# Block products of the first MLP: stores on ScalarE's queue, modulation products in the up stage, two buffers for table products, entry loads with places of their own

## The chip, the cores and the metric

The kernel runs on one core of one Trainium2 chip. Its time is device microseconds of one execution; three runs of the kernel before took 3001.24, 3002.39 and 3007.51 us (median 3002.39 us). One more execution was profiled; every duration below comes from it.

## What is computed

Two layers over 1024 latent tokens and 256 context tokens, model width 1024, MLP width 4096, all in float32. Layer 0 mixes tokens by differential attention, layer 1 by a bidirectional S5 state-space layer. Each mixer is followed by a squared-ReLU MLP; each sub-layer has an RMSNorm before and after, and a shift, scale and gate ("modulation") that come from the conditioning vectors. The part that matters here, cut from the reference:

```python
mod_l = jnp.einsum('bd,de->be', sc, ada_w[i]) + ada_b[i]        # six segments of 1024
h = rmsnorm(x, norm_g[i, 2]) * (1.0 + s2) + sh2
x = x + g2 * rmsnorm(sqrelu_mlp(h, mlp_w1[i], mlp_w2[i]), norm_g[i, 3])
# next layer: h = rmsnorm(x, norm_g[1, 0]) * (1.0 + s1) + sh1, then the S5 mixer
def sqrelu_mlp(h, w1, w2):
    return jnp.einsum('btf,fd->btd', jnp.square(jax.nn.relu(jnp.einsum('btd,df->btf', h, w1))), w2)
```

## The kernel before

A float32 product is made as three TensorE products of split operands (high times high, high times low, low times high; `mm3`, L132 to L134). The split is a ScalarE copy (L137) and a VectorE subtraction (L138). All DMAs but a few at the start are issued by SyncE, through the helper at L80, in one queue in program order.

The program is written stage by stage, but a scheduler with a timing model of its own then lays out each engine's instructions: an instruction goes where that model has it ready, not where the code emits it. Background work is given as generators in `self.bg`; `step()` advances the first of them.

**Up stage** (`mlp0_up`). The hidden width is done in pairs of 128-column blocks, by products of sums (Strassen's scheme: seven products `A11, S1, S2, S4, S3, A12, A22` for a pair instead of eight). ScalarE copies and squares, VectorE adds. For the blocks from `CONV` = 8 on, the hidden blocks and their sums are stored to `Hd[0..6]`, 84 stores of 320 KB: 12 pairs times seven kinds. Beside it GpSimd forms the sums of the rows of `mlp_w2` (L1546 to L1549, `sum_rows`): two row blocks are loaded, combined, and stored to `Td`. In the background stands `ada(0, 5)`: for one modulation segment eight loads of 512 KB, four small matmuls each (L208), then the end of the segment (L222 to L236); and `rows_out` (L286 to L288), which writes the layer's modulation to `rowd` in DRAM.

**Down stage** (`mlp0_start`, `mlp0_blocks`, `mlp0_down`). 84 block products ("ops") are worked off. Each has a load from `Hd` and one from `mlp_w2` or `Td` into one of a few raw places (`oraw`, `op_load`), a split into one of 14 slots (`op_prepare`), and 15 matmuls. Places and slots lie in tiles H, W, RW and RD; RW and RD get their memory only when the up stage's pool is free. After the ops come the groups of the plain hidden blocks (`mlp0_group`, additions L1497). When both parts of a token tile are added, `m0_tile` runs its end: ScalarE squares (L1830), the products with modulation rows (L1831), the residual (L1842), the modulation (L1850); then four transposes (L1817) put it into U, which the S5 layer reads. The rows come from `rowd`.

In the background of the down stage stand `s5_phases`, then `s5_tables` (32 steps: loads, VectorE and GpSimd products, transposes on TensorE at L1189 and their copy L1190, a product L1199, its copy L1201 into `Ks`, and every second step four stores of `Ks` to `kd`), with four `lags`, each of which issues 32 DMAs from `ktd` to `recd`; then `ada(1, 0)`, `ada(1, 1)` and `rows_out(1)`. After each unit of ops `step` is called (L1711), and `mlp0_down` drains what is left. The first S5 product is at L1925 and needs U and the tables in `recd`.

Of the kernel before, what the change touches and what calls it, by code (L numbers as in the profile page):

```python
# [6 lines left out]
F32 = mybir.dt.float32  # L7
F32R = mybir.dt.float32r
I32 = mybir.dt.int32
AF = mybir.ActivationFunctionType  # L10
# [60 lines left out]
class Prog:  # L71
# [140 lines left out]
    def ada_steps(self, l, seg, acc, raw):  # L212
        for k in range(8):
            w = raw.next()
            self.ada_load(w, l, seg, k)
            self.ada_product(w, k, acc)
            yield
        self.ada_end(l, seg, acc)
        yield

# [929 lines left out]
    def s5_tables(self, o, w, acc):  # L1150
# [9 lines left out]
        t4, t2, Ks = shaped(t, (4, 9, 16)), shaped(t[:, 0:512], (4, 8, 16)), self.wv(w + 7, 2, 128)  # L1160
# [34 lines left out]
        def products(i):  # L1195
            tb_, W, q = ins[i % 4][2], Wr[i % 3], todo[i]
            d, x0 = q // 16, 4 * q
            for j in range(4):
                nc.tensor.matmul(acc[32 * j : 32 * j + 32, 0:128], tb_[:, j],  # L1199
                                 W[:, j, d : d + 8].rearrange("p i c -> p (i c)"), start=True, stop=True)  # L1200
            nc.scalar.activation(Ks[:, q % 2], acc[:, 0:128], AF.Copy)  # L1201
            if q % 2:
                for j in range(4):
                    dst = self.kd[x0 - 4 : x0 + 4].rearrange("(y j) c n -> j c y n", j=4)[j]
                    self.dma(dst, Ks[32 * j : 32 * j + 16])
# [323 lines left out]
    def mlp0_up(self):  # L1529
# [5 lines left out]
        self.bg = [self.ada(0, 5, acc), self.rows_out(0, acc)]  # L1535
# [5 lines left out]
        def store(n, p, t):  # L1541
            self.dma(self.Hd[self.KINDS.index(n)][p - self.CONV // 2], t)

        def sum_rows(p):
            (b11, b12), (b21, b22) = ((r[:, 0:512], r[:, 512:1024]) for r in rows)
            g(b11, b12, b11, ALU.subtract)  # L1546
            g(b12, b22, b12, ALU.subtract)
            g(b22, b22, b11, ALU.subtract)
            g(b21, b21, b22, ALU.subtract)  # L1549
            for j in range(2):  # L1550
                self.dma(self.Td[p - self.CONV // 2, j], rows[j])

        for p in range(self.HEAD // 2, 16):
            conv = 2 * p < self.CONV
            if p < 15:
                for j in range(2):
                    self.dma(rows[j], self.I["mlp_w2"][0, 128 * (2 * p + 2 + j) : 128 * (2 * p + 2 + j) + 128])
# [3 lines left out]
            for j in range(2):  # L1561
# [7 lines left out]
                while later:  # L1569
                    later.pop(0)()  # L1570

            def emit(j, gr, t):
# [28 lines left out]
                if (j, gr) == (1, 1) and p < 15:  # L1601
                    sum_rows(p + 1)
# [8 lines left out]
    def mlp0_start(self):  # L1611
# [11 lines left out]
        self.raw = Ring([self.fv(40, 1024), self.fv(44, 1024)])  # L1623
        acc = self.bank(3)
        self.bg = [self.s5_phases(40), self.s5_tables(40, 0, acc)] + [self.ada(1, seg, acc) for seg in (0, 1)]
        self.bg.append(self.rows_out(1, acc))
# [8 lines left out]
        slots = [h(x, 2304) for x in (71, 62, 53, 44, 26, 17, 35, 8)] + [rd(9 * i, 2304) for i in range(6)]  # L1635
# [6 lines left out]
        for k, q in self.ops:  # L1642
            r = next(x for x in last if x is not spare or k in ("S1", "S2", "S3", "A22"))
# [7 lines left out]
    def op_load(self, i):  # L1651
# [8 lines left out]
        else:  # L1660
            f = self.CONV + 2 * q + (k != "A11")
            b = self.I["mlp_w2"][0, 128 * f : 128 * f + 128]
            h = int(k == "S4")
        self.dma(r[:, 640:1152], b[:, 512 * h : 512 * h + 512])
# [24 lines left out]
    def mlp0_blocks(self):  # L1689
# [15 lines left out]
        def unit():  # L1705
# [5 lines left out]
            self.step(2 if u % 5 in (0, 2) else 1)  # L1711
# [632 lines left out]
    def run(self):  # L2344
        tc = self.tc
        pool = lambda name, **kw: tc.tile_pool(name=name, bufs=1, **kw)
        with pool("cst") as self.cst, pool("psp", space=bass.MemoryType.PSUM) as psp, \
# [13 lines left out]
            self.Hd = [dt(f"Hd{i}", 16 - self.CONV // 2, 128, 640) for i in range(7)]  # L2361
            self.Td = dt("Td", 16 - self.CONV // 2, 2, 128, 1024)
# [39 lines left out]
            with pool("fd") as fp:  # L2402
                self.F = fp.tile([128, 56 * KB], F32, name="FD")
                with pool("rd") as rp:
                    self.RD, self.RW = rp.tile([128, 56 * KB], F32R, name="RD"), rp.tile([128, 9 * KB], F32, name="RW")
# [58 lines left out]
```

## Time and profile before

| | before |
|---|---|
| median of three runs | 3002.39 us |
| the profiled execution | 2996.76 us |
| its span | 2994.9 us |
| TensorE busy | 2773.5 us (93%) |
| VectorE, ScalarE, GpSimd busy | 1929.4, 1391.4, 1133.3 us |
| HBM read, written | 385.10, 178.88 MB |

Times in the trace are microseconds from the start of the span. The up stage with its pairs stands at about 1071 to 1417 us, the ops from 1417 to 1762, the end of the tables to 1798, the groups of plain blocks from 1805 to 1924, the first S5 product at 1972. A row of the timeline gives start, duration, engine, line, operation, output <- input, and in brackets how long the engine was idle before it and what ended that. ACTq and SPq are the instruction queues of ScalarE and SyncE.

### The profile page before, as it was taken

Reading aid. Unit: us, or ns where it says so; the run is one execution under the profiler, and the core shown is the slowest. Engines: PE = TensorE matmul, PEld = TensorE weight load, DVE = VectorE, ACT = ScalarE, POOL = GpSimd, SP = SyncE. Lnnn points to the kernel's source line nnn. Section 1 sums busy time; section 2 is a strip of 40 time slices with the busy share of each in tenths; the row PEclk is TensorE's granted clock in tenths of the full one; section 3 lists DMA queues with packets and bytes.
Section 4 is the critical chain, followed back from the end, with each engine's and each line's share of the span. In section 5 each row is a group of like instructions: output and inputs, shape, how many; then the busy total and the mean of one; then the engine's idle time right before and its main releaser. Section 6 shows DMA issues by size and latency. Waiting matters only on the chain.

```text
span 2994.9 us, 44339 instructions
## 1 busy us (share of the span) xinstructions
PE 2773.5 (93%) x15864; PEld 2297.7 (77%) x15864; DVE 1929.4 (64%) x2744; ACT 1391.4 (46%) x2488; POOL 1133.3 (38%) x991
## 2 busy tenths in 40 slices
PE   7999999999889999999999969659899999999999
PEld 5687888888778877887777746558888778888887
DVE  5457888888744565554787653578734576658566
ACT  3325565556545644454443331256534655334443
POOL 2314666677555223300211010478502323336323
PEclk9999999999899999999999979879999999999999
DMA  9964445545627467634878766569944366457544
GB/s 275 300 197 144 130 150 159 155 155 160 214 68 203 124 215 270 233 135 145 275 233 254 225 190 194 153 185 262 317 141 151 137 218 197 155 191 275 164 137 140
DMA packets 446280, 571.15 MB, mean 191 GB/s; under 512 B 59254, under 2 KB 300396, under 8 KB 444908
## 3 DMA queue, kind: packets, MB, share of 16 engines
q1 hardware_dynamic: 445676, 566.22, 60.1%
q10 hardware_dynamic: 384, 2.10, 0.3%
q8 instruction: 125, 2.05, 0.3%
q14 instruction: 95, 0.78, 0.1%
HBM read 385.10 MB, written 178.88 MB: 188 GB/s over the span
## 4 chain that ended last, share of the span: by engine, by line
PE 31%; DMA 7%; DVE 5%; SPq 3%; issue 2%; ACT 2%; POOL 1%; DVEq 0%; POOLq 0%; ACTq 0%
PE PS L132 9%; PE PS L133 9%; PE PS L134 9%; SPq L80 3%; PE PS L1925 1%; DMA W<-in_mlp_w 1%; PE PS L1966 1%; DVE H L138 1%; DVE FD L1945 1%; DMA RW<-in_mlp_w 1%; DMA W<-Ad 1%; DMA H<-hidd 1%; DMA RW<-Td 0%; PE PS L270 0%; DMA Pd<-R 0%
## 5 line engine op out<-in xcount | busy, mean ns | idle before, releaser
L132 PE MATMUL PS<-H 128*128 128x512 f32 x768 | 297.6, 395 | 13.7 <-ACT H L137 13.0
L133 PE MATMUL PS<-H 128*128 128x512 f32 x768 | 302.6, 394 | 1.7 <-DVE H L138 1.7
L134 PE MATMUL PS<-H 128*128 128x512 f32 x768 | 301.3, 393 | 0.8 <-DVE H L138 0.8
L132 PE MATMUL PS<-H,R 128*128 128x512 f32 (+1 forms) x784 | 290.8, 374 | 9.7 <-DVE FC L487 5.5
L133 PE MATMUL PS<-H,R 128*128 128x512 f32 (+1 forms) x784 | 282.9, 361 | 1.4 <-POOL H L138 1.4
L134 PE MATMUL PS<-H,R 128*128 128x512 f32 (+1 forms) x784 | 283.1, 362 | 0.0
L138 DVE TENSOR_TENSOR H<-W,H 128x512 fp32r<-128x512 f32 (+2 forms) x150 | 146.4, 983 | 126.0 <-ACT H L137 117.9
L571 ACT ACTIVATE F<-F,stat 128x1280 f32<-128x1280 f32 x128 | 174.4, 1362 | 98.8 <-DVE F L561 98.5
L132 PE MATMUL PS<-R,H 128*128 128x512 f32 x540 | 216.4, 402 | 2.2 <-ACT R L137 1.7
L133 PE MATMUL PS<-R,H 128*128 128x512 f32 x540 | 212.3, 393 | 0.0
L134 PE MATMUL PS<-R,H 128*128 128x512 f32 x540 | 211.6, 395 | 0.0
L137 ACT ACTIVATE H<-W 128x512 fp32r<-128x512 f32 (+3 forms) x171 | 114.4, 676 | 201.3 <-PE PS L133 116.2
L137 ACT ACTIVATE R<-W 128x512 fp32r<-128x512 f32 (+1 forms) x178 | 127.4, 720 | 170.1 <-PE PS L133 87.2
L561 DVE TENSOR_SCALAR_CACHE_REDUCE F<-PS 128x1280 f32<-128x1280 f32 x128 | 185.1, 1482 | 13.9 <-PE PS L536 13.8
L608 POOL TENSOR_SCALAR R<-F 128x256 fp32r<-128x256 f32 (+1 forms) x128 | 135.5, 1058 | 149.4 <-ACT F L607 135.6
L132 PEld LDWEIGHTS PS<-H 128*128 128x128 f32 x768 | 144.9, 189 | 47.0 <-ACT H L137 15.2
L132 PEld LDWEIGHTS PS<-H,R 128*128 128x128 f32 x784 | 148.1, 189 | 37.0 <-DVE FC L487 7.2
L536 PE MATMUL PS<-R,R 64*128 64x256 f32 (+1 forms) x1440 | 159.2, 349 | 16.1 <-DVE F L561 9.9
L133 PEld LDWEIGHTS PS<-H 128*128 128x128 f32 x768 | 145.6, 190 | 34.5 <-DVE H L138 3.3
L134 PEld LDWEIGHTS PS<-H 128*128 128x128 f32 x768 | 145.5, 190 | 31.7 <-DVE H L138 1.3
L138 DVE TENSOR_TENSOR R<-W,R 128x512 fp32r<-128x512 f32 (+1 forms) x142 | 126.9, 898 | 64.6 <-ACT R L137 56.2
L134 PEld LDWEIGHTS PS<-H,R 128*128 128x128 f32 x784 | 148.4, 189 | 24.4 <-POOL R L138 1.4
(491 smaller groups left out, 7433.0 us busy)
## 6 DMA issues: line engine op xcount, KB each, us to landing
W<-in_mlp_w SPq DMA_DIRECT2D x204, 256.0 KB
Ad<-F SPq DMA_DIRECT2D x112, 256.0 KB
W<-Ad SPq DMA_DIRECT2D x112, 256.0 KB
Hd<-FU SPq DMA_DIRECT2D x84, 320.0 KB
W<-in_ada_w SPq DMA_DIRECT2D x34, 512.0 KB
U<-in_ada_w SPq DMA_DIRECT2D x32, 512.0 KB
W<-in_s_w_glu SPq DMA_DIRECT2D x64, 256.0 KB
RW<-Hd SPq DMA_DIRECT2D x47, 320.0 KB
```

What stands on the lines that cost most here:

```text
L80: return self.nc.sync.dma_start(out=out, in_=in_)
L132: mm(out, ah, bh, start=first, stop=False, **kw)
L133: mm(out, ah, bl, start=False, stop=False, **kw)
L134: mm(out, al, bh, start=False, stop=last, **kw)
L137: self.nc.scalar.activation(hi, src, AF.Copy)
L138: (lo_eng or self.nc.vector).tensor_tensor(lo, src, hi.bitcast(F32), ALU.subtract)
L536: mm(self.PS[:, o : o + k1 - k0], Q[rows, i, qs], K[j][rows, k0:k1], start=n == 0, stop=n == 2)
L561: ts(p[c], self.PS[:, 1280 * c : 1280 * c + 1280], 1.0, None, ALU.mult, ALU.min, accum_out=sm[:, c : c + 1])
L571: nc.scalar.activation(p[c], p[c], AF.Exp, bias=sm[:, c : c + 1], scale=-1.0, accum_out=sn[:, 0:1] if c else s0[:, u + 1 : u + 2])
L608: nc.gpsimd.tensor_scalar(hi, t, 1.0, 0.0, ALU.mult, ALU.add)
L1925: mm(b[:, o : o + 160], X[:, d, i, 64 * j : 64 * j + 128], U[:, 4 * n + i, cols], start=True, stop=True)
L1945: v.tensor_tensor_scan(t2, r, t1, 0.0, ALU.mult, ALU.add)
```

## The change

Five edits, all in layer 0's MLP and what runs beside it:

- The stores of hidden blocks and sums (84) and of row sums (24) are issued by ScalarE instead of SyncE. The row loads for the next pair are asked for at a pair's first finished block (of four), the sums formed at its last, the stores issued in the next pair. Two raw rows are also saved to a new tensor `Bd`.
- `ada(0, 5)` becomes `ada_late`, which loads one step ahead into its one buffer; `ada(1, 0)`, `ada(1, 1)` and `rows_out(1)` move from the down stage to the up stage.
- `Ks` has two buffers, used in turn by pairs of table steps; RW grows by 1 KB per partition for it.
- Ops 1 and 2 get raw places in H, not in RW, and load from `Bd`; the slots are used in another order.
- Background work in the down stage is stepped 5 times in 4 units instead of 7 in 5.

```diff
+    def ada_late(self, l, seg, acc):
+        w = self.raw.next()
+        self.ada_load(w, l, seg, 0)
+        for k in range(8):
+            yield
+            self.ada_product(w, k, acc)
+            if k < 7:
+                self.ada_load(w, l, seg, k + 1)
+        self.ada_end(l, seg, acc)
...
-        t4, t2, Ks = shaped(t, (4, 9, 16)), shaped(t[:, 0:512], (4, 8, 16)), self.wv(w + 7, 2, 128)
+        t4, t2, Ks = shaped(t, (4, 9, 16)), shaped(t[:, 0:512], (4, 8, 16)), [self.wv(w + 7, 2, 128), self.view(self.RW, 9, (2, 128))]
...
-            nc.scalar.activation(Ks[:, q % 2], acc[:, 0:128], AF.Copy)
+            nc.scalar.activation(Ks[q // 2 % 2][:, q % 2], acc[:, 0:128], AF.Copy)
...
-                    self.dma(dst, Ks[32 * j : 32 * j + 16])
+                    self.dma(dst, Ks[q // 2 % 2][32 * j : 32 * j + 16])
...
-        self.bg = [self.ada(0, 5, acc), self.rows_out(0, acc)]
+        self.bg = [self.ada_late(0, 5, acc), self.rows_out(0, acc)] + [self.ada_late(1, seg, acc) for seg in (0, 1)]
+        self.bg.append(self.rows_out(1, acc))
...
         def store(n, p, t):
-            self.dma(self.Hd[self.KINDS.index(n)][p - self.CONV // 2], t)
+            self.nc.scalar.dma_start(out=self.Hd[self.KINDS.index(n)][p - self.CONV // 2], in_=t)
...
         def sum_rows(p):
             (b11, b12), (b21, b22) = ((r[:, 0:512], r[:, 512:1024]) for r in rows)
+            if p - self.CONV // 2 in (1, 2):
+                self.nc.scalar.dma_start(out=self.Bd[p - self.CONV // 2 - 1], in_=b11)
...
+        def rows_store(p):
             for j in range(2):
-                self.dma(self.Td[p - self.CONV // 2, j], rows[j])
+                self.nc.scalar.dma_start(out=self.Td[p - self.CONV // 2, j], in_=rows[j])
...
+                if j == 0 and not conv:
+                    rows_store(p)
...
-                if (j, gr) == (1, 1) and p < 15:
+                if (j, gr) == (0, 1) and p < 15:
+                    rows_load(p + 1)
+                if (j, gr) == (1, 0) and p < 15:
                     sum_rows(p + 1)
...
-        self.bg = [self.s5_phases(40), self.s5_tables(40, 0, acc)] + [self.ada(1, seg, acc) for seg in (0, 1)]
-        self.bg.append(self.rows_out(1, acc))
+        self.bg = [self.s5_phases(40), self.s5_tables(40, 0, self.bank(3))]
...
-        slots = [h(x, 2304) for x in (71, 62, 53, 44, 26, 17, 35, 8)] + [rd(9 * i, 2304) for i in range(6)]
+        slots = [h(x, 2304) for x in (71, 62, 17, 8, 26, 35, 44, 53)] + [rd(9 * i, 2304) for i in range(6)]
...
+            if i == 2:
+                self.oraw.append(h(40, 1152).bitcast(F32))
+                continue
+            r = next(x for x in last if x is not spare or i == 1 or k in ("S1", "S2", "S3", "A22"))
+            if i == 1:
+                r = spare
...
+            if i in (1, 2):
+                b = self.Bd[i - 1]
...
-            self.step(2 if u % 5 in (0, 2) else 1)
+            self.step(2 if u % 4 == 0 else 1)
```

How the built programs differ, at two places. TensorE, the end of the background work beside the ops, before: L1189 are a table step's transposes, L1199 its products, L208 a modulation product, L132 the first matmuls of the plain groups.

```order
L1199 MATMUL PS<-W,FD 32x128 x4
L1189 MATMUL PS<-ident,FD 128x128 x4
L1199 MATMUL PS<-FD,W 32x128 x4
L1189 MATMUL PS<-ident,FD 128x128 x4
L1199 MATMUL PS<-FD,H 32x128 x4
L208 MATMUL PS<-FD,scT 32x256 x4
L132 MATMUL PS<-RD,H 128x512 x6
```

These are the last of eight products that stand behind the last op with nothing between them. After, TensorE, behind the 63rd op; transposes are now L1199 and table products L1209:

```order
L1209 MATMUL PS<-W,FD 32x128 x4
L1199 MATMUL PS<-ident,FD 128x128 x4
L1209 MATMUL PS<-FD 32x128 x4
L1199 MATMUL PS<-ident,FD 128x128 x4
L1209 MATMUL PS<-FD,W 32x128 x4
L1199 MATMUL PS<-ident,FD 128x128 x4
L1209 MATMUL PS<-W,H 32x128 x4
L132 MATMUL PS<-H 128x512 x5
```

The chain at the end has gone. Bare chains stand inside the ops instead: four products here, three behind the 45th op with six matmuls between them, one later; the last table product stands 90 matmuls ahead of the end of the ops. On SyncE the DMAs of the first and second lags stand behind the loads of the 48th and 63rd op (before: the 48th and 72nd), the third's behind the 72nd (before: behind all 84); from the phases' load at the entry to the load of the last op SyncE issues 524 DMAs (before: 450).

VectorE, at the end of the groups, before: L1497 is the last addition of a tile, L1831, L1842 and L1850 are the parts of a tile's end, L1817 its transposes; these are the first rows from the last addition on.

```order
L1497 TENSOR_TENSOR FD<-PS,FD 128x1024
L1850 SCALAR_TENSOR_TENSOR FD<-FD,tl,W 128x1024
L1842 SCALAR_TENSOR_TENSOR FD<-FD,tl,H 128x1024
L1831 TENSOR_TENSOR U<-FD,W 128x1024
L1817 STREAM_TRANSPOSE U<-FD 128x16x32 x4
```

After, all of VectorE's rows from the last addition (now L1507) to the S5 layer; L1856, L1867, L1875 and L1842 are the lines above in the same order as products, residual, modulation, transposes:

```order
L1507 TENSOR_TENSOR FD<-PS,FD 128x1024
L1875 SCALAR_TENSOR_TENSOR FD<-U,tl,W 128x1024
L1856 TENSOR_TENSOR U<-FD,W 128x1024
L1867 SCALAR_TENSOR_TENSOR FD<-W,tl,H 128x1024
L1875 SCALAR_TENSOR_TENSOR FD<-U,tl,W 128x1024
L1867 SCALAR_TENSOR_TENSOR FD<-U,tl,H 128x1024
L1856 TENSOR_TENSOR W<-FD,W 128x1024
L1842 STREAM_TRANSPOSE U<-FD 128x16x32 x4
L1856 TENSOR_TENSOR U<-FD,W 128x1024
L1875 SCALAR_TENSOR_TENSOR FD<-W,tl 128x1024
L1875 SCALAR_TENSOR_TENSOR FD<-U,tl,W 128x1024
L1842 STREAM_TRANSPOSE U<-FD 128x16x32 x4
```

Before, seven modulations, six residuals, five products with rows and sixteen transposes stood behind the last addition; after, four, two, three and eight.

More of the change, by code (lines that the diff above doesn't have):

```diff
@@ L1549, in sum_rows, with rows_load @@
             g(b21, b21, b22, ALU.subtract)
+        def rows_store(p):
             for j in range(2):
-                self.dma(self.Td[p - self.CONV // 2, j], rows[j])
+                self.nc.scalar.dma_start(out=self.Td[p - self.CONV // 2, j], in_=rows[j])
+        def rows_load(p):
+            for j in range(2):
+                self.dma(rows[j], self.I["mlp_w2"][0, 128 * (2 * p + j) : 128 * (2 * p + j) + 128])
         for p in range(self.HEAD // 2, 16):
             conv = 2 * p < self.CONV
-            if p < 15:
-                for j in range(2):
-                    self.dma(rows[j], self.I["mlp_w2"][0, 128 * (2 * p + 2 + j) : 128 * (2 * p + 2 + j) + 128])
             w = self.pair_weights([self.load1(0, 2 * p + j, raw) for j in range(2)],
@@ L1622, in mlp0_start @@
         self.yb = Ring([self.PS[:, x : x + 1024] for x in (2048, 3072, 0)])
-        self.raw = Ring([self.fv(40, 1024), self.fv(44, 1024)])
-        acc = self.bank(3)
-        self.bg = [self.s5_phases(40), self.s5_tables(40, 0, acc)] + [self.ada(1, seg, acc) for seg in (0, 1)]
-        self.bg.append(self.rows_out(1, acc))
+        self.bg = [self.s5_phases(40), self.s5_tables(40, 0, self.bank(3))]
         self.w2 = {}
@@ L1641, in mlp0_start @@
         last = raws + [spare]
-        for k, q in self.ops:
-            r = next(x for x in last if x is not spare or k in ("S1", "S2", "S3", "A22"))
+        for i, (k, q) in enumerate(self.ops):
+            if i == 2:
[4 more added lines that the diff above has]
+                r = spare
             last = [x for x in last if x is not r] + [r]
@@ L2361, in run @@
             self.Hd = [dt(f"Hd{i}", 16 - self.CONV // 2, 128, 640) for i in range(7)]
+            self.Bd = dt("Bd", 2, 128, 512)
             self.Td = dt("Td", 16 - self.CONV // 2, 2, 128, 1024)
@@ L2404, in run @@
                 with pool("rd") as rp:
-                    self.RD, self.RW = rp.tile([128, 56 * KB], F32R, name="RD"), rp.tile([128, 9 * KB], F32, name="RW")
+                    self.RD, self.RW = rp.tile([128, 56 * KB], F32R, name="RD"), rp.tile([128, 10 * KB], F32, name="RW")
                     self.mlp0_start()
```

## Prediction

> **What bounds the kernel now.** I read the page first, then the busy time of each engine in the stretches that the change touches, then TensorE's waits, then the timelines at the places where TensorE stands. In the rows below stand a stretch, its length, the busy time (and instructions) of TensorE, its weight loads, VectorE, ScalarE and GpSimd, the granted clock, the DMA share and GB/s.
>
> ```profile
> 1071.00:1250.00 179.00, 166.86 (x893) 138.97 (x891) 102.68 (x124) 78.93 (x149) 71.20 (x48) 0.98 0.80 268
> 1250.00:1400.00 150.00, 147.52 (x778) 127.31 (x777) 79.80 (x114) 74.86 (x137) 0.00 (x0) 0.99 0.41 139
> 1417.00:1432.70 15.70, 7.25 (x16) 4.48 (x15) 4.29 (x5) 3.51 (x4) 5.32 (x8) 0.57 0.84 275
> 1432.70:1761.90 329.20, 319.20 (x1562) 250.38 (x1560) 247.47 (x287) 131.54 (x170) 49.08 (x36) 0.98 0.80 245
> 1761.90:1805.30 43.40, 11.02 (x81) 5.40 (x81) 16.23 (x23) 6.58 (x14) 5.10 (x4) 0.56 0.61 160
> 1805.30:1923.60 118.30, 118.30 (x587) 89.63 (x587) 44.37 (x47) 15.97 (x25) 27.13 (x22) 0.99 0.58 173
> 1923.60:1972.20 48.60, 0.04 (x1) 0.02 (x1) 41.45 (x43) 23.58 (x36) 33.26 (x32) 0.54 0.67 189
> ```
>
> TensorE bounds all of this but four places. Up to 1250 it stands 12.1 of 179 us. At the entry of the down stage 15.7 us pass with 16 matmuls. Behind the ops 43.4 us pass with 11.0 busy, at a granted clock of 0.56. Behind the groups it does nothing for 48.6 us. From 1250 to 1400 and in the groups it is full, so work taken off another engine there is worth nothing.
>
> **The change, part by part.**
>
> *Entry (slots, raw places).*
>
> ```profile
> 1416.75 0.40 PE L133 MATMUL PS<-H 128*128 128x512 f32 x1
> 1416.98 0.39 PE L134 MATMUL PS<-H 128*128 128x512 f32 x1
> 1424.36 1.22 PE L132 MATMUL PS<-H 128*128 128x512 f32 x2 [6.98 <-ACT H L137]
> 1426.77 0.63 PE L133 MATMUL PS<-H 128*128 128x512 f32 x1
> ...
> 1423.92 0.32 SPq L80 DMA_DIRECT2D RW<-Hd  x1
> ...
> 1427.90 1.16 ACT L137 ACTIVATE H<-RW 128x1152 fp32r<-128x1152 f32 x1 [3.60 <-DMA RW<-in_mlp_w]
> ```
>
> The first two rows start 0.23 us apart, the pace at full clock, so 16 of them are 3.6 us and the entry loses 12.1 us: three ops wait for raw places, and RW is loaded only from 1423.92. Ops 1 and 2 no longer need RW. Ops 0 to 2 are 45 matmuls, 10.2 us. RW still opens some 7 us after the last matmul, its load takes 4.0 us to the split, the split 1.16 us and the subtraction about as much: op 3 at 13 us. The entry then loses 3 to 4 us. I take a gain of 8 us (bounds 3 and 11).
>
> *Table products (two `Ks`, steps, ada out of the way).*
>
> ```profile
> 1756.11 19.60 SPq L80 DMA_DIRECT2D recd<-ktd  x32
> ...
> 1780.06 0.28 ACT L1201 ACTIVATE W<-PS 128x128 f32<-128x128 f32 x1 [16.38 <-DMA kd<-W]
> ...
> 1783.10 0.69 DVE L1181 TENSOR_TENSOR FD<-FD 128x512 f32<-128x512 f32 x1 [14.22 <-DMA FD<-tbd]
> ...
> 1761.45 0.43 PE L1199 MATMUL PS<-FD 128*32 128x128 f32 x8
> 1780.39 1.11 PE L1189 MATMUL PS<-ident,FD 128*128 128x128 f32 x4 [16.23 <-ACT W L1201]
> 1783.35 1.12 PE L1189 MATMUL PS<-ident,FD 128*128 128x128 f32 x4 [0.46 <-ACT W L1201]
> 1805.30 2.93 PE L132 MATMUL PS<-RD,H 128*128 128x512 f32 x6 [3.39 <-ACT RD L137]
> ```
>
> A lag's 32 DMAs hold SyncE's queue for 19.6 us, and ScalarE's copy of a table product waits behind them for `kd` to be stored out of its only buffer. VectorE waits for a load in the same queue, so the second buffer alone would leave 14.2 of the 16.4 us. What removes the stall is the order: the chain is spread into the ops. Its useful work, about 6 us at full clock, stays, so 37 of the 43.4 us are at stake. The price is paid elsewhere. A bare transpose and product take 2.96 us. The first chain (three pairs, 1.4 us of matmuls between) costs 10 us, half for VectorE's share of a step (bounds 6 and 18). The second (four products, three transposes) costs 9 us, and the next op's load stands on SyncE behind a lag and a table store that waits for this chain: 7 more. Is SyncE's queue the next to be late?
>
> ```profile
> 1547.30 0.72 SPq L80 DMA_DIRECT2D W<-Hd  x1
> 1589.34 0.42 SPq L80 DMA_DIRECT2D RW<-Hd  x1
> ...
> 1461.87 1.05 PE L1189 MATMUL PS<-ident,FD 128*128 128x128 f32 x4
> 1759.77 0.94 PE L1189 MATMUL PS<-ident,FD 128*128 128x128 f32 x4
> ```
>
> The first row is the load of the 48th op, the second of the 49th: 42.0 us without a load, and TensorE hardly stood. By the program the two transposes stand 9.4 and 85.0 ops in, so an op with its share of tables takes 3.94 us, and the split slots hold 14 ops, 55 us. That covers one lag. After, op 49 comes a few DMAs later still, op 50 another 22 DMAs later (11 us at some 0.5 us each, between the 0.42 and 0.72 of these rows), and from op 64 to op 84 SyncE issues 152 DMAs, about 79 us, for 20 ops that need 79: no reserve is left. I add 6 us there (bounds 0 and 25). Total price 10 + 16 + 6 = 32 us, of which I count 9 against the 10 us that TensorE idles in the ops now, since those waits are for the same loads (a choice; without it the gain is 5). Gain: 37 - 32 + 9 = 14 us (bounds +30 and -10).
>
> *Modulation moved.*
>
> ```profile
> 1821.23 0.64 PE L208 MATMUL PS<-FD,scT 128*32 128x256 f32 x8
> ...
> PE PS L132 <- ACT FU L1466: 10.2, 3, 5.4
> PE PS L132 <- ACT H L137: 8.3, 2, 7.0
> PE PS L208 <- DMA FU<-in_ada_w: 4.4, 4, 1.9
> ```
>
> The 16 moved groups of four products cost 0.64 us each in either stage: 10 us out, 10 us in, zero. Their 16 loads (8.4 MB) go too. In the up stage, a product is 4 to 10 us after its load and waited 4.4 us for eight; 24 with the load a step ahead: the same 4 us.
>
> What moving them frees is the end of the token tiles:
>
> ```profile
> 1897.96 1.03 ACT L1830 ACTIVATE PS<-FD 128x1024 f32<-128x1024 f32 x1 [46.56 <-DVE adat L288]
> ...
> 1932.90 1.24 DVE L1497 TENSOR_TENSOR FD<-PS,FD 128x1024 f32<-128x1024 f32 x1
> ...
> 1967.49 4.14 SPq L80 DMA_DIRECT2D W<-recd  x4
> ...
> 1972.21 4.03 PE L1925 MATMUL PS<-U,H 128*128 128x160 f32 x16 [48.57 <-DMA W<-recd]
> ...
> L1817 DVE STREAM_TRANSPOSE U<-FD 128x512 f32<-128x512 f32 x16 | 10.0, 677 | 0.0
> L1850 DVE SCALAR_TENSOR_TENSOR FD<-FD,tl,W 128x1024 f32<-128x1024 f32 x3 | 3.8, 1277 | 3.6 <-ACT PS L1830 2.5 <-POOL tl L144 1.0
> L1842 DVE SCALAR_TENSOR_TENSOR FD<-FD,tl,H 128x1024 f32<-128x1024 f32 x2 | 2.5, 1274 | 0.0
> L1831 DVE TENSOR_TENSOR W<-FD,W 128x1024 f32<-128x1024 f32 x1 | 1.2, 1225 | 0.0
> ```
>
> ScalarE waits 46.6 us for the last modulation rows, which come at 1898; six of ten tiles stand fully added ahead of them in the program. All ten ends are pressed behind it, and VectorE adds the last tile only at 1932.90. With the rows ready, the ends run beside the groups, where VectorE is busy 44 of 118 us. By the program four modulations, two residuals, three products and eight transposes stand behind the last addition: 4 x 1.28 + 2 x 1.27 + 3 x 1.23 + 8 x 0.63 = 16.4 us; the addition is 1.24, and 2 to 3 us go into ScalarE's squares and GpSimd's root of the last tile. The gap becomes about 20 us, a gain of 28 (bounds 18 and 33). The wait for `recd` is not the cause: those four loads are issued last because their places in W hold the rows.
>
> *ScalarE's queue, row sums.*
>
> ```profile
> SPq L80 <- POOL FU L1547: 36.2, 12, 4.8
> SPq L80 <- POOL W L1549: 9.8, 4, 3.0
> ...
> ACT R L137 <- DMA W<-in_mlp_w: 38.9, 5, 12.2
> ...
> 5.02 1.92 ACTq L315 DMA_DIRECT2D F<-in_x  x3
> ```
>
> Weight loads no longer stand behind stores, so part of ScalarE's 38.9 us of waiting goes. But 110 DMAs at 0.64 us are 70 us of its queue, and the waits for GpSimd's sums, 46.0 us, move from SyncE to ScalarE, with the weight splits and PSUM copies queued behind them and TensorE behind those. ScalarE is busy 79 of 179 us; I take a gain of 3 of the 12.1 us (bounds +12 and -15). The Trainium skill ("DMA: Bandwidth & Descriptors", Rules for kernel authors) says that spreading DMAs over issuing engines brings no bandwidth and saves only issue time; by it this term would be nothing and the sum 3 us worse. No run here shows which.
>
> *Start of the groups.* Their weights now queue on SyncE behind the last op loads: -3 us (bounds 0 and -6). It replaces the 3.39 us wait above, which stood in the 37.
>
> Sum: 8 + 14 + 0 + 28 + 3 - 3 = 50 us. The profiled execution took 2996.8 us, so 2947; the median of the runs is 5.6 us over it, so **2952 us**.
>
> **The rivals.**
>
> (a) *SyncE's queue becomes the bound in the ops.* For it: the 152 DMAs for 20 ops, and three lags among the ops where there were two. Against: the queue also waits for free places, so it has slack in the first half. The chains and the queue then cost all of the 37 + 10 us and 10 more: the tables lose 10 instead of gaining 14, 2976 us.
>
> (b) *The gap before S5 stays long*, because the third and fourth lag, the `xb` stores and the `recd` loads queue late. For it: 1967.49 above. Against: VectorE ends only at 1972. The gap shortens by 10 instead of 28: 2970 us.
>
> (c) *Slower: a store holds ScalarE.* 24 row stores wait 46.0 us for GpSimd, and the issues take 70 us of the queue. TensorE has a margin of one product, 12 matmuls or 2.7 us, before the copy it needs. If all of the 46 us and a third of the 70 reach TensorE, 69 us are lost; from 53 us on (the other terms' sum of 47, and 0.2%) the kernel is slower; 69 gives 3002.4 - 47 + 69 = 3024 us. The Trainium skill ("TensorE: Matmul & The Clock Gate", its table of specifications) calls ScalarE's queue strictly first in, first out; the trace agrees where the copy at 1780.06 held TensorE for 16.23 us. Against: the stores stand where the scheduler has their sums ready, and ScalarE is idle for half of the stage.
>
> (d) *No change*: (a) and (b) together and 8 us more lost on ScalarE, 24 + 18 + 8 = 50.
>
> **How the numbers follow.** Forecast 0.70 (own range 2930 to 2968, from terms that rarely miss together), (a) 0.11, (b) 0.07, (d) 0.04, (c) 0.08. Range 2928 to 2985: it takes in (a) and (b) and leaves out (c), (d) and the corner where all terms gain. A measurement of this kernel can tell about 0.2% (6 us) from no change: faster 0.88, same 0.04, slower 0.08.
>
> **What would show it.** Right: the first op within 1 us of the last up matmul; no stretch of 30 us without ops before the groups, but two of some 10 us behind ops 45 and 63; ScalarE's first L1855 before the last group's middle; the gap before the first S5 product near 20 us; TensorE's idle time in the pairs not above 12 us. Wrong: the gap near 40 us, op loads that land when TensorE already waits for more than 30 us in all, or ScalarE's waits for GpSimd followed by TensorE's.

## The result, and the profile after

The changed kernel takes 2969.93 us in the median of four executions (2964.33 to 2975.51), 0.9889 of the kernel before [0.9866, 0.9911]; a second measurement (e5 below) gave 0.9903 [0.9888, 0.9918]. By these ratios that is 29 to 33 us faster. 50 us and 2952 us were forecast: the sign is right, the time lies in the range, and the gain is about six tenths of what was forecast. The profiled execution took 2975.51 us (span 2973.7), the slowest of the four, where that of before (2996.76) was faster than its median; between these two alone lie 21 us.

Both programs issue the same 512-column matmuls on TensorE, and their order differs only inside the stages. So the two traces can be laid side by side by count: find the start of the n-th such matmul in each, from the same one at 1030 us, and subtract. The table gives the time that each stage took by this count, in us; "again" is e5, a second profile of the changed kernel. The expectations of the experiments were written from an earlier count by merged rows, which differs from this one by up to 2 us.

| stage (512-column matmuls) | before | after | again |
|---|---|---|---|
| pairs of the up stage (1187) | 371.8 | 378.7 | 375.3 |
| entry of the down stage (140) | 45.5 | 44.8 | 44.7 |
| ops (1148) | 298.6 | 344.8 | 342.2 |
| end of the ops to the first group (60) | 66.2 | 13.6 | 13.6 |
| groups (438) | 111.2 | 106.5 | 107.3 |
| gap to the first S5 product | 49.0 | 28.4 | 28.3 |
| sum | 942.2 | 916.7 | 911.3 |

To the first S5 product 25.5 us are gained, in the second profile 30.9. The S5 products behind it take about 176 us in both; the rest of the difference (5 us lost) lies in later stages that the change does not touch.

Two numbers carry the table. 53 us behind the ops have gone, the stall of 43.4 us and the waits and the half pace on both sides of it, but the ops before it are 44 to 46 us longer. And the gap before S5 is 21 us shorter, not 28. The stretches of the changed kernel (start and end, length, busy time of TensorE, its weight loads, VectorE, ScalarE and GpSimd, clock, DMA share, GB/s):

```profile
1425.30:1439.40 14.10, 4.10 (x19) 3.05 (x17) 3.98 (x5) 4.49 (x5) 7.10 (x9) 0.72 0.58 188
1439.40:1676.00 236.60, 226.72 (x1111) 175.76 (x1112) 171.63 (x196) 88.12 (x111) 37.69 (x29) 0.97 0.76 230
1676.00:1797.70 121.70, 96.70 (x470) 72.57 (x469) 76.44 (x98) 37.11 (x53) 13.82 (x11) 0.87 0.79 233
1797.70:1811.00 13.30, 13.30 (x60) 11.04 (x59) 6.17 (x9) 8.32 (x12) 0.00 (x0) 1.00 1.04 327
1811.00:1918.40 107.40, 102.96 (x443) 84.22 (x441) 67.96 (x67) 32.26 (x51) 36.90 (x35) 0.97 0.49 149
1918.40:1946.40 28.00, 0.01 (x1) 0.04 (x1) 22.57 (x22) 12.08 (x20) 21.11 (x20) 0.58 0.64 197
```

The third row is the new place: 121.7 us with 25.0 idle and the clock at 0.87. TensorE has no long wait there, only many of up to 5.5 us, the longer ones followed by matmuls at half pace. By TensorE's waits, 15.1 of the 25.0 us are for splits of op loads (L137, L138) and 9.8 are inside the chains of table products. Why the splits are late is read from SyncE's queue beside it:

```profile
1654.96 0.84 SPq L80 DMA_DIRECT2D RW<-Hd  x1
...
1656.35 19.42 SPq L80 DMA_DIRECT2D recd<-ktd  x32
...
1692.02 0.50 SPq L80 DMA_DIRECT2D RW<-Hd  x1
...
1697.77 2.50 PE L132 MATMUL PS<-H 128*128 128x512 f32 x5 [1.63 <-ACT H L137]
...
1725.15 0.58 SPq L80 DMA_DIRECT2D RW<-Hd  x1
...
1726.31 19.41 SPq L80 DMA_DIRECT2D recd<-ktd  x32
...
1730.46 1.22 PE L132 MATMUL PS<-H 128*128 128x512 f32 x2 [5.49 <-ACT H L137]
...
1748.15 1.08 SPq L80 DMA_DIRECT2D H<-Hd  x1
```

The `RW<-Hd` and `H<-Hd` rows are op loads. Between the first two lie 37.1 us without one, between the next two 23.0. A lag (the rows of 32) and the table DMAs that queued up behind it fill these times. A split (L137) that TensorE waits for is late because its load was asked for late. The row of 1697.77 also shows a second cost: behind a thin stretch five matmuls take 2.50 us, where they take 1.1 us at full pace.

### The profile page after: what moved, and what is told of

It reads as the page before. It is cut to its first block, busy times and chain, and to the rows that moved or that the text cites. A ratio compares the mean times of both kernels' runs of the same rounds, so it can differ in the third digit from the quotient of the medians.

```text
span 2973.7 us, 44326 instructions
## 1 busy us (share of the span) xinstructions
PE 2773.8 (93%) x15864; PEld 2296.3 (77%) x15864; DVE 1925.4 (65%) x2744; ACT 1394.1 (47%) x2488; POOL 1128.0 (38%) x991
## 5 line engine op out<-in xcount | busy, mean ns | idle before, releaser
L132 PE MATMUL PS<-H 128*128 128x512 f32 x768 | 298.7, 397 | 22.2 <-ACT H L137 22.2
L132 PE MATMUL PS<-H,R 128*128 128x512 f32 (+1 forms) x784 | 292.4, 375 | 10.5 <-DVE FC L497 5.5
L132 PE MATMUL PS<-R,H 128*128 128x512 f32 x540 | 215.8, 401 | 1.9 <-ACT R L137 1.4
L138 DVE TENSOR_TENSOR H<-W,H 128x512 fp32r<-128x512 f32 (+2 forms) x145 | 138.2, 961 | 109.1 <-ACT H L137 105.0
L137 ACT ACTIVATE H<-W 128x512 fp32r<-128x512 f32 (+3 forms) x166 | 108.4, 661 | 208.4 <-PE PS L133 116.8
L137 ACT ACTIVATE R<-W 128x512 fp32r<-128x512 f32 (+1 forms) x178 | 126.9, 719 | 152.3 <-PE PS L133 77.7
L132 PEld LDWEIGHTS PS<-H 128*128 128x128 f32 x768 | 145.5, 190 | 55.5 <-ACT H L137 24.5
L132 PEld LDWEIGHTS PS<-H,R 128*128 128x128 f32 x784 | 148.9, 190 | 40.0 <-DVE FC L497 7.1
L138 DVE TENSOR_TENSOR R<-W,R 128x512 fp32r<-128x512 f32 (+1 forms) x142 | 126.8, 900 | 79.7 <-ACT R L137 71.8
L546 PE MATMUL PS<-R,R 64*128 64x256 f32 (+1 forms) x1440 | 157.6, 346 | 15.6 <-DVE F L571 9.4
```

What stands on the lines that cost most here:

```text
L132: mm(out, ah, bh, start=first, stop=False, **kw)
L137: self.nc.scalar.activation(hi, src, AF.Copy)
L138: (lo_eng or self.nc.vector).tensor_tensor(lo, src, hi.bitcast(F32), ALU.subtract)
L546: mm(self.PS[:, o : o + k1 - k0], Q[rows, i, qs], K[j][rows, k0:k1], start=n == 0, stop=n == 2)
```

## The experiments

Each kernel is the changed one with the edit shown, profiled once and timed in five rounds beside the kernel before; ratios are to the kernel before. Stages are by the count of matmuls as above.

**e1: the modulations back in the down stage.**

```diff
-        self.bg = [self.ada_late(0, 5, acc), self.rows_out(0, acc)] + [self.ada_late(1, seg, acc) for seg in (0, 1)]
-        self.bg.append(self.rows_out(1, acc))
+        self.bg = [self.ada_late(0, 5, acc), self.rows_out(0, acc)]
...
-        self.bg = [self.s5_phases(40), self.s5_tables(40, 0, self.bank(3))]
+        self.bg = [self.s5_phases(40), self.s5_tables(40, 0, acc)] + [self.ada(1, seg, acc) for seg in (0, 1)]
+        self.bg.append(self.rows_out(1, acc))
```

> The changed kernel with one part undone: the two modulation segments and the row store that follows them stand in the down stage again. By the built program TensorE's and SyncE's order is that of the changed kernel up to the last op. Theory of the prediction: moving the modulations gained nothing by itself (10 us out, 10 us in) and freed the end of the token tiles, 28 us; undone, the gap ahead of the first S5 product is 45 to 50 us again, the up stage is 10 us shorter, and the time goes from 2970 to about 2998. What the two traces say when they are laid side by side by the count of matmuls: the gap went from 48.6 to 28.0, so this part is worth about 20 us: 2990. Rival: the gap is set by the loads of recd or by VectorE's own work, not by the modulation rows: the gap stays near 28 and the time within 5 us of 2970.

Measured: 2985.99 us, 0.9946 [0.9928, 0.9963]; up stage 369.3 us, groups 117.3, gap 36.5. So the move is worth 15 to 16 us by the medians (13 to 17 by the ratios), about half of the whole gain, but not 28: the gap went back by 8 us, not by 20. The groups are longer by 10 to 11 us with the products in them, while the up stage is shorter by only 6 to 9. TensorE's waits in the pairs of e1 (total, times, longest) say why the products cost less there than their 10 us:

```profile
PE PS L132 <- ACT FU L1476: 10.8, 4, 4.4
```

and in the changed kernel:

```profile
PE PS L208 <- DMA FU<-in_ada_w: 7.4, 5, 3.9
PE PS L132 <- ACT FU L1476: 1.3, 2, 0.7
```

Without the products TensorE waits 10.8 us for ScalarE's copies; with them 1.3 us. Part of the moved work fills a wait that was there before.

**e2: the stores of the up stage on SyncE.**

```diff
-            self.nc.scalar.dma_start(out=self.Hd[self.KINDS.index(n)][p - self.CONV // 2], in_=t)
+            self.dma(self.Hd[self.KINDS.index(n)][p - self.CONV // 2], t)
```

and the same for `Bd` and `Td`.

> The changed kernel with the 84 stores of hidden blocks and sums, the two row copies and the 24 row sums issued by SyncE again. By the built program nothing else moves. Theory of the prediction: the stores on ScalarE's queue gain 3 us, so 2973; the traces' count gives 3.6 us for the up stage (6.4 us later at its end although 10 us of modulation products were added). Rival by a page's rule (another queue saves issue time alone): 2970, no difference in the up stage. Rival by which a store holds ScalarE: the up stage gets shorter by 5 us or more, below 2965. Third possibility: with the modulation loads now in the up stage too, SyncE's queue would hold them behind the stores, and TensorE waits there for them: 2975 to 2985.

Measured: 2964.87 us, 0.9883 [0.9865, 0.9902], the changed kernel's time; up stage 372.4 us. In the nine profiles with these stores on ScalarE and the modulations in the up stage it takes 373.4 to 380.2 us, in the three with them on SyncE (e2, e7, e12) 372.4 to 377.2. The 3 us forecast are not there.

**e3: the entry undone**, with the rows saved to `Bd` and the loads from it.

```diff
-        slots = [h(x, 2304) for x in (71, 62, 17, 8, 26, 35, 44, 53)] + [rd(9 * i, 2304) for i in range(6)]
+        slots = [h(x, 2304) for x in (71, 62, 53, 44, 26, 17, 35, 8)] + [rd(9 * i, 2304) for i in range(6)]
...
-            if i == 2:
-                self.oraw.append(h(40, 1152).bitcast(F32))
-                continue
-            r = next(x for x in last if x is not spare or i == 1 or k in ("S1", "S2", "S3", "A22"))
-            if i == 1:
-                r = spare
+            r = next(x for x in last if x is not spare or k in ("S1", "S2", "S3", "A22"))
```

> The changed kernel with the entry of the down stage undone: raw places and slots in the old order, no rows saved to the extra tensor. By the built program this also spreads the table products evenly through the ops again, with the second lag behind the 72nd op and the third behind the last, and five pairs of transposes and products behind the last op. Theory of the prediction: the entry is worth 8 us, and the table layout with the chains inside is the better one: 2978 to 2992. What the traces say: the entry was worth only 1 us, and the stretch from the 63rd to the 80th op lost 35 us to SyncE's queue, which this layout does not; it pays a chain of five pairs behind the ops, 15 to 25 us: 2955 to 2965, faster than the changed kernel.

Measured: 2960.72 us, 0.9871 [0.9851, 0.9891]; entry 43.9 us, ops 297.2, end of the ops 56.0, gap 24.0. Undone, the entry is no longer than with the change. With the tables spread as in the kernel before, the ops are as short as they were (298.6), and a stall is behind them again. That together is 9 to 10 us less than the changed kernel's median, at the edge of what the intervals tell apart. In this kernel the largest single wait of the stall is one lag. In SyncE's queue and on TensorE:

```profile
1757.52 19.58 SPq L80 DMA_DIRECT2D recd<-ktd  x32
1777.20 1.79 SPq L80 DMA_DIRECT2D kd<-W  x4
...
1782.92 0.65 PE L1209 MATMUL PS<-FD 128*32 128x128 f32 x8 [15.90 <-ACT FD L1200]
```

**e4: one buffer and the old steps.**

```diff
-        ..., Ks = ..., [self.wv(w + 7, 2, 128), self.view(self.RW, 9, (2, 128))]
+        ..., Ks = ..., self.wv(w + 7, 2, 128)
...
-            self.step(2 if u % 4 == 0 else 1)
+            self.step(2 if u % 5 in (0, 2) else 1)
```

> The changed kernel with one buffer for table products and the old stepping of the background work. By the built program the second lag stands behind the 69th op and the third behind the last, and five pairs of table products stand behind the ops, each second one waiting for the one buffer to be stored. Theory of the prediction: the table part is worth 14 us; undone, the stall behind the ops is back, with 37 us at stake: about 2984. What the traces say: the table part gave back in the ops nearly all that it saved behind them (46 us longer ops against 43 us of stall), so undone the time stays at 2965 to 2975; the ops are 15 to 30 us shorter, and 20 to 35 us stand behind them.

Measured: 2960.33 us, 0.9863 [0.9842, 0.9884]; ops 308.3 us, end of the ops 47.7. So it is the changed kernel's time or 10 us less, not 14 more. The table part, as it was made, is worth nothing or a little less than nothing.

**e5: the changed kernel again**, beside the next three.

> The changed kernel as it is, beside the next three on the same chip, so that differences of a few us between them can be read. 2964 to 2972, as before.

Measured: 2970.57 us, 0.9903 [0.9888, 0.9918].

**e6: the table stores on ScalarE**, which makes the copies that are stored.

```diff
-            self.dma(X[:, :, 0:128], Xs)
-            self.dma(X[:, :, 128:192], Xs[:, :, 0:64])
+            nc.scalar.dma_start(out=X[:, :, 0:128], in_=Xs)
+            nc.scalar.dma_start(out=X[:, :, 128:192], in_=Xs[:, :, 0:64])
...
-                    self.dma(dst, Ks[q // 2 % 2][32 * j : 32 * j + 16])
+                    nc.scalar.dma_start(out=dst, in_=Ks[q // 2 % 2][32 * j : 32 * j + 16])
```

> The changed kernel with the stores of the table steps (64 of the transposes' copies to recd and 64 of the products to kd) issued by ScalarE, which makes both copies itself, so that it waits for nothing there. SyncE issues 399 DMAs from the phases' load to the last op load instead of 524, the second lag stands behind the 69th op, the third behind the 79th, and nothing of the tables is left behind the ops. Theory now: SyncE's queue is the bound of the ops from the 63rd on, where the changed kernel lost 35 us and more; taken off it, 25 to 40 us come back: 2930 to 2945. Theory of the prediction as it stood: the price lies in the bare chains of transposes and products (10 and 9 us) as much as in the queue; the chains here are shorter, so 10 to 15 us: 2955 to 2960. Rivals: the DMA engines' share or the loads' own time bound the ops, and nothing changes: 2965 to 2972; or 128 issues of some 0.6 us make ScalarE late for the splits: above 2975.

Measured: 2955.09 us, 0.9853 [0.9834, 0.9872]; ops 332.3 us, end of the ops 17.9, groups 99.5. 15 us come back, less than the 25 expected. Against e5 the stretch in the ops is only 10 us shorter and the end of the ops 4 us longer; the groups give 8. What is left in the ops, from SyncE's queue and TensorE of e6:

```profile
1723.34 0.33 SPq L80 DMA_DIRECT2D H<-Hd  x1
...
1725.16 24.84 SPq L80 DMA_DIRECT2D recd<-ktd  x32
...
1755.59 0.41 SPq L80 DMA_DIRECT2D RW<-Hd  x1
...
1761.74 2.50 PE L132 MATMUL PS<-H 128*128 128x512 f32 x5 [4.71 <-ACT H L137]
```

Still 32.2 us without an op load. With 128 stores fewer in the queue, the gap stays as long as a lag, here 24.84 us, and what waits behind it. So the number of issues (524 or 399) was not the whole cause; the lag as one block is the next suspect, which e9 tests.

**e7: e6 with the stores of the up stage on SyncE.**

```diff
-            self.nc.scalar.dma_start(out=self.Hd[self.KINDS.index(n)][p - self.CONV // 2], in_=t)
+            self.dma(self.Hd[self.KINDS.index(n)][p - self.CONV // 2], t)
```

> The run before with the stores of the up stage issued by SyncE again: the queue that is free in the up stage serves there, and ScalarE's serves the tables in the ops. The ops keep the order of the run before. Theory now: the stores on ScalarE cost the up stage 3 to 6 us (the up stage took 371.9 us to its end with the stores on SyncE, 374.9 to 379.3 with them on ScalarE), so 3 to 6 us below the run before. Theory of the prediction: 3 us above it. Rival (issue time alone): the same.

Measured: 2954.22 us, 0.9852 [0.9833, 0.9871]: e6's time. My expectation of 3 to 6 us fell; the differences of the up stage between profiles were spread.

**e8: the loads of the first S5 phase on ScalarE.**

```diff
-            self.dma(t, self.ptd[:, c0 : c0 + 128 * w].rearrange("p (d x w) -> p d x w", d=2, w=w)[:, :, 0:4])
+            nc.scalar.dma_start(out=t, in_=self.ptd[:, c0 : c0 + 128 * w].rearrange("p (d x w) -> p d x w", d=2, w=w)[:, :, 0:4])
```

The expectation rests on these rows of the changed kernel (GpSimd's, then VectorE's, whose last row is the last four transposes):

```profile
1915.24 1.28 POOL L1933 TENSOR_TENSOR FD<-H 128x640 int32<-128x640 int32 x1 [8.69 <-DMA H<-ptd]
1916.47 2.40 POOL L1856 TENSOR_TENSOR U<-FD,W 128x1024 f32<-128x1024 f32 x1
...
1920.09 2.34 POOL L1856 TENSOR_TENSOR U<-FD,W 128x1024 f32<-128x1024 f32 x1
...
1924.19 1.28 DVE L1867 SCALAR_TENSOR_TENSOR FD<-U,tl,H 128x1024 f32<-128x1024 f32 x1 [4.17 <-POOL tl L144]
...
1930.74 1.22 DVE L1507 TENSOR_TENSOR FD<-PS,FD 128x1024 f32<-128x1024 f32 x1
...
1945.47 2.49 DVE L1842 STREAM_TRANSPOSE U<-FD 128x512 f32<-128x512 f32 x4
```

> The changed kernel with one edit behind the groups: the two loads that the first S5 phase product on GpSimd (L1933) waits for are issued by ScalarE, not by SyncE behind nine loads of residual rows. In the trace of the changed kernel GpSimd stood 8.7 us for them, with the tiles' products and roots queued behind, VectorE waited 4.2 us for a root, and the last addition came 12 us after the last matmul. Theory: this wait is why the gap ahead of S5 is 28 us and not 20; without it the gap is 20 to 23 us and the time 5 to 8 us below the changed kernel. Rival: VectorE's own queue of tile ends sets the gap, or GpSimd's products (2.4 us each) do, and the gap stays at 26 to 29 us.

Measured: 2965.28 us, 0.9895 [0.9877, 0.9913]; gap 26.9 us. The rival holds: the load was early, and the last addition still came 12.8 us after the groups' end, because GpSimd's products themselves stand ahead of the roots:

```profile
1906.06 3.40 POOL L1856 TENSOR_TENSOR U<-FD,W 128x1024 f32<-128x1024 f32 x1 [2.29 <-DVE FD L1507]
...
1909.81 2.40 POOL L1856 TENSOR_TENSOR U<-FD,W 128x1024 f32<-128x1024 f32 x1
...
1912.75 1.28 DVE L1867 SCALAR_TENSOR_TENSOR FD<-U,tl,H 128x1024 f32<-128x1024 f32 x1 [2.05 <-POOL tl L144]
```

**e9: e6 with three lags behind the tables.**

```diff
-            if i > 1 and i % 8 == 1:
-                yield from lags(i // 8 - 1)
+            for c in {9: [0], 33: [1, 2, 3]}.get(i, ()):
+                yield from lags(c)
```

> The run with the table stores on ScalarE (e6), and the second, third and fourth lag emitted behind the last table step instead of after each eighth step. By the built program one lag stands in one piece behind the 48th op, as in all, and no other in one piece ahead of the last op; the next two lie behind the last op loads, the last in the groups, and five pairs of transposes and products stand behind the ops with no lag among them. Theory now: what still bounds the ops from the 63rd on in e6 is the lag as one block of 32 issues, 20 us in which SyncE sends no op load; without it the ops run as in the kernel before (298 us from the 21st op's place to the end of the ops instead of 330), the five pairs cost 15 to 22 us, and the sum is 10 to 20 us below e6: 2935 to 2945. Rival: the lags only move, and block the loads of the plain groups instead: the groups lose what the ops gain, 2950 to 2960.

Measured: 2948.70 us, 0.9844 [0.9826, 0.9862]; ops 301.7 us, end of the ops 41.8, groups 103.7, gap 24.5. The stretches of e9 that answer to the third to the last of the changed kernel:

```profile
1660.00:1749.80 89.80, 89.80 (x456) 70.97 (x455) 69.23 (x91) 32.74 (x49) 13.30 (x8) 1.00 0.83 252
1749.80:1790.80 41.00, 23.64 (x138) 16.13 (x137) 19.02 (x27) 10.99 (x22) 4.57 (x4) 0.72 0.71 201
1790.80:1898.80 108.00, 105.51 (x456) 86.55 (x454) 65.72 (x65) 30.92 (x48) 41.25 (x38) 0.98 0.49 149
1898.80:1923.00 24.20, 0.12 (x1) 0.03 (x1) 21.81 (x21) 10.76 (x17) 16.70 (x17) 0.54 0.70 207
```

In the first row TensorE is full, at a DMA share of 0.83, above the 0.79 of the changed kernel's bad stretch: the DMA engines were not the bound there, SyncE's order was. And the 32 DMAs of the second lag do stand in that row, from 1658 to 1698, but in twelve pieces of one to five with op loads and table DMAs between them:

```profile
1671.18 3.29 SPq L80 DMA_DIRECT2D recd<-ktd  x5
1675.39 0.32 SPq L80 DMA_DIRECT2D H<-Hd  x1
```

Issued in pieces there, the same DMAs cost TensorE nothing. The ops are 31 us shorter than in e6. 28 of these go back: 24 to the end of the ops, where the five pairs stand, and 4 to the groups. The end of the ops takes 28 us more than without pairs. The pairs themselves take 20.1 us of that (1762.50 to 1782.58), as expected; the rest is mostly a wait of 4.92 us for the first group's split, which ScalarE begins at 1786.40, behind a table store (1785.82) and a copy (1786.23) in its own queue, and half pace behind it. In the groups TensorE's one wait is 2.49 us for a VectorE addition, and not for a load, as the rival had it.

**e10: the last four tiles' products on VectorE.**

```diff
-            squares(G, v if i in (6, 7) else pool)
+            squares(G, v if 4 <= i < 8 else pool)
...
-            squares(A, v if i % 2 or i == 6 else pool)
+            squares(A, v if i % 2 or 4 <= i < 8 else pool)
```

> The changed kernel with the products of the last four token tiles with their rows on VectorE (1.2 us each) and none on GpSimd (2.4 us each). Nothing ahead of the groups' end moves in the built program. Theory: the gap ahead of S5 is 28 us and not 20 because GpSimd is the late engine there: in e8 it had its phase loads in time and still worked without a pause from 1906 to 1925 us, three products of 2.3 to 3.4 us with the roots queued behind them, and the last addition came 12.8 us after the groups' end as before. Without the products the roots come at once, and the gap is 21 to 24 us, the time 4 to 7 us below the changed kernel: 2963 to 2967. Rival: VectorE has no room for three more products, and the gap stays at 27 to 29 us.

Measured: 2965.83 us, 0.9898 [0.9877, 0.9919]; gap 25.1 us. Between the two: 3 us, too little for the times to tell.

**e11: e9, e8 and e10 together.** The edits are those above.

> All that helped, on the changed kernel: table stores on ScalarE, three lags behind the tables (as e9), the phase loads on ScalarE (e8) and the last four tiles' products on VectorE (e10). Theory: the terms add. e9 measured 2949; the gap ahead of S5, 24.4 us there, goes to 20 to 23 us: 2944 to 2948. Rival: the gap is already at what VectorE's own tile ends take, and it stays at 2947 to 2952.

Measured: 2948.05 us, 0.9833 [0.9817, 0.985]; gap 23.0 us, as expected, but not told from e9 by the times. VectorE has no pause of note left between the groups' last matmul at 1899.0 and the last transposes:

```profile
1906.71 1.21 DVE L1507 TENSOR_TENSOR FD<-PS,FD 128x1024 f32<-128x1024 f32 x1
...
1919.81 1.29 DVE L1875 SCALAR_TENSOR_TENSOR FD<-U,tl,W 128x1024 f32<-128x1024 f32 x1 [0.19 <-issue]
1921.13 2.49 DVE L1842 STREAM_TRANSPOSE U<-FD 128x512 f32<-128x512 f32 x4
```

**e12: e11 without two of the five edits**, the entry (as e3) and the stores on ScalarE (as e2).

> The run before with two of the five edits undone: the entry (raw places, slots, the extra tensor) and the stores of the up stage, which SyncE issues again. By the built program six pairs of table products stand behind the ops instead of five. Theory now: these two edits are worth nothing that can be measured (the 140 matmuls across the entry took 43.9 us undone in e3 and 45.2 to 45.8 us with it; the up stage was no longer with the stores on SyncE), so the time is that of e11 within 4 us. Theory of the prediction: 8 us for the entry and 3 us for the stores are lost: 2955 to 2960.

Measured: 2944.86 us, 0.9825 [0.9809, 0.9841]; up stage 377.2 us, entry 44.0, ops 295.1, end of the ops 44.9, groups 102.5, gap 24.2. This is the lowest median of all, 53 us below the kernel before, measured beside it, and 25 below the changed one's, without the two edits; the intervals don't tell it from e11.

## Why the prediction was right, and where its sizes were wrong

The forecast's mechanisms decided the sign: the rows for the token tiles come early, and no stall stands behind the ops. The step that failed is the cost of the tables in the ops, and with it the cover at the entry and the engine counted for the tail. Term by term:

**Entry, +8: under 1, and as much without the edit (e3).** In the changed kernel RW opens late for the same reason as before, and the three ops do not cover the time:

```profile
1418.81 0.39 PE L134 MATMUL PS<-H 128*128 128x512 f32 x1
1419.03 1.07 PE L132 MATMUL PS<-H 128*128 128x512 f32 x4
...
1422.66 0.39 PE L132 MATMUL PS<-H,RT 128*128 128x512 f32 x1
...
1425.15 0.39 PE L134 MATMUL PS<-H,RT 128*128 128x512 f32 x1
...
1429.01 0.39 PE L134 MATMUL PS<-H 128*128 128x512 f32 x1
1439.40 2.50 PE L132 MATMUL PS<-H 128*128 128x512 f32 x5 [10.01 <-ACT H L137]
...
1433.49 0.32 SPq L80 DMA_DIRECT2D RW<-Hd  x1
...
1438.19 1.16 ACT L137 ACTIVATE H<-RW 128x1152 fp32r<-128x1152 f32 x1 [3.56 <-DMA RW<-in_mlp_w]
```

The rows that read H and RT are the last product of the up stage. 16 matmuls of the ops run ahead of it, from 1419.03, and only 17 behind it, up to 1429.2; the forecast put 45 behind it, 10.2 us. (The other 12, of op 0, stand still further ahead inside the up stage, in the kernel before too.) The wall, RW, opens 8 us after that product (7 were taken), and the work meant to cover it had been spent ahead. I had taken the ops' place from the text of the program; the order in which TensorE's instructions stand would have shown it. "The first op within 1 us of the last up matmul" was fulfilled and meant nothing.

**Table products, +14: 6 to 9 us, and less than other placements give.** The stall was sized rightly: 53 us went from the stretch behind the ops, about 1 us of it modulation products; less the chain's 6 us of useful work that is 46, and the forecast had 37 and 9. But the ops pay 44 to 46 us. The first chain cost less than the 10 us taken: the 60 matmuls across it take 23.9 and 21.4 us, 17.6 in the kernel before and 15.6 in e3, where no chain stands there. The rest is 37 us against the kernel before, over the 240 matmuls from the 63rd op on (101.9 us against 64.6). Of these, 14.5 are the second chain and 23 what comes behind it; in the forecast stood 9 for this chain, 7 for the starved load and 6 for the queue. So the term that was mis-sized is the queue behind the second chain: 23 us, where 13 were taken. The bound of 25 us for the queue was right in kind and just wide enough.

What was missed is that a lag is a block: the queue's mean reserve (79 us of issues for 79 us of ops) says nothing when one lag is 20 us in one piece and each op load behind it waits for the whole piece. e6 (fewer issues, same block) and e9 (no second or third block in the ops, TensorE full) show it. A block cost little where enough ops were loaded when it began. By the count of loads and products, 13 and 12 ops stood ready at the two lags among the ops of the kernel before (1559.8, 1656.9), and its gaps of 42.0 and 31.8 us without an op load left the ops' pace as it was. In the changed kernel 12 stood ready at the first lag, but only 7 at the second (1656.3) and 4 at the third (1726.3); in e6 it was 12, 12 and 5 (1725.2), and behind the third its ops lose most. That this reserve decides is read from these traces; no run varied it alone.

The rival (a) was this mechanism at a price of 10 more; it came true in the ops, and the other terms kept the time below its 2976.

**Modulation moved, 0: better than that.** 10 us left the down stage, and the up stage with all its edits is 3 to 7 us longer, since the products fill waits for ScalarE (e1).

**End of the token tiles, +28: 21.** ScalarE begins the tiles in time, and the wait for the rows is gone:

```profile
1860.67 1.03 ACT L1855 ACTIVATE PS<-FD 128x1024 f32<-128x1024 f32 x1 [1.89 <-DVE FD L1507]
```

The count of what stands behind VectorE's last addition was right (16.4 us and 1.24 for the addition forecast; 1930.74 to 1946.39 is 15.7). The addition itself was put right behind the groups, and it comes 12 us later, held by tile ends ahead of it on VectorE, and these in part by GpSimd's roots and products: with GpSimd relieved the gap is 25.1 us (e10) and 23.0 (e11), and there VectorE's own queue fills it. e1 shows that 8 us of the 21 hang on the moved modulations; the other 12 come with the remaining edits, and no run takes them apart.

**ScalarE's queue, +3: nothing** (e2, e7). The sentence of the Trainium skill ("DMA: Bandwidth & Descriptors", Rules for kernel authors) by which spreading DMAs over issuing engines brings no bandwidth and only saves issue time agrees with both runs (0.9883 against 0.9889, 0.9852 against 0.9853). Its other half fits e6: where SyncE had no issue time to spare, 128 stores on the other queue gave 15 us, though the lags moved in SyncE's order there too. The rival (c), a store that holds ScalarE, did not come: TensorE's waits for ScalarE's copies in the pairs were 10.2 us before, 10.8 with the stores on ScalarE and the modulations left in the down stage (e1), and 1.3 in the changed kernel.

**Start of the groups, -3: -7 to -8, and later than thought.** The groups begin at full pace, but the fourth lag blocks the next weights:

```profile
1810.73 19.42 SPq L80 DMA_DIRECT2D recd<-ktd  x32
1830.26 0.87 SPq L80 DMA_DIRECT2D W<-in_mlp_w  x2
...
1834.08 1.06 ACT L137 ACTIVATE H<-W 128x1024 fp32r<-128x1024 f32 x1 [20.78 <-DMA W<-in_mlp_w]
...
1839.47 0.77 PE L132 MATMUL PS<-H,RD 128*128 128x512 f32 x1 [4.43 <-issue]
```

ScalarE waits 20.8 us for a load that SyncE did not ask for before the end of the lag; TensorE stands 4.4 us and runs at half pace behind it. The trace names no releaser for this wait ("issue"); that it is this load is read from the order of the rows, and from e6, where two of these loads stand ahead of the lag and the wait is not there. 438 matmuls at 0.227 us are 99.4 us; the groups take 106.5, in e6 99.5.

Of the signs named: no stretch of 30 us without ops, ScalarE's first L1855 early, idle time in the pairs about 10 us, all as said; the gap of 28 lies between "near 20" and "near 40"; the two stalls of some 10 us cost 4 to 6 us and 14.5, and 23 us more were spread over the 100 us behind the second.

Open: whether all lags in pieces would keep their early places without the block, as the second lag of e9 does in a later place, and whether the lags could go on GpSimd's queue; neither was tried.

## What to carry to other kernels

A queue's reserve is not the sum of its issues against the time of the stage: look for the longest block in it, ask who is queued behind, and count what is already loaded when the block begins. Work moved from a stall into a busy stage costs nothing only as long as the queue that feeds that stage is not the one that the work needs. And of an overlap, read on the waiting engine itself whether the covering work stands behind the point where the wall begins.

## What the runs showed of the hardware

A lag's small DMAs hold SyncE's queue longer than the large loads do: 32 of them take 19.42 us, 0.61 us each, where most loads of 128x512 or 128x640 words take 0.32 to 0.48.

And a thin stretch costs TensorE more than its waits. These are rows of the changed kernel, in the columns of the stretches above:

```profile
1714.86:1718.27 3.41, 1.82 (x12) 0.75 (x12) 3.41 (x8) 1.51 (x3) 0.60 (x1) 1.00 0.99 330
1718.27:1721.68 3.41, 3.17 (x10) 2.58 (x11) 3.25 (x5) 1.66 (x4) 0.00 (x0) 0.50 0.85 234
```

In the first TensorE works 1.82 of 3.41 us, with no wait above 1.45 us; in the second the granted clock is 0.50. Behind 1684.14:1687.55, with 1.08 us of work, it is at 0.50 for longer, and five matmuls take 2.50 us at 1697.77 instead of 1.1. So 121.7 us with 25.0 us of idle time went by at a mean clock of 0.87. The Trainium skill ("TensorE: Matmul & The Clock Gate", Part 1: The HAM clock gate) has the clock go to half after an idle window of some 3.4 us; here it went to half behind stretches of that length in which the engine was partly busy.
